# Attention logits of a pair of heads in the two row halves of TensorE, without copied q and k

## The chip, the cores and the metric

The kernel runs on one core of a Trainium2 chip. The metric is the device time of one execution in microseconds (us); lower is better. Times of several runs are given as a median with the lowest and the highest.

## What is computed

A trunk of two decoder layers on 512 tokens of width 1024. Each layer is a mixer (attention) and a SwiGLU feed-forward, each behind an RMS norm and with a residual add. Layer 0 mixes with 16 heads of width 64, 8 of them with a merged dilated-window pattern and 8 plainly causal at this length. Layer 1 is differential attention: 8 heads, each with two maps of queries and keys of width 64 and values of width 128. Of it the part that matters here is this:

```
qh = q.reshape(B, S, H, 2, HEAD_DIM).transpose(0, 2, 3, 1, 4)
kh = k.reshape(B, S, H, 2, HEAD_DIM).transpose(0, 2, 3, 1, 4)
...
logits = jnp.einsum('bhiqd,bhikd->bhiqk', qc, kh).astype(jnp.float32) * ATTN_SCALE
logits = jnp.where(kpos[None, :] <= qpos[:, None], logits, NEG_INF)
p = jax.nn.softmax(logits, axis=-1)
attn = p[:, :, 0] - lam * p[:, :, 1]
```

## The kernel before

Everything is kept transposed, features on the 128 partitions and the 512 tokens along the free dimension. Each large operand is split into a high and a low part (float32r), and a product of two operands is made of three matmuls: high by high, high by low and low by high (`mm3`, line 420). The `z` of a tile's shape `[128, 2, 512]` is that part.

**Weights** arrive as slabs of 128 x 1024. A slab lands raw in `wraw` (2 buffers) by a transfer of SP's queue. ScalarE writes the high part to `whl`, and the low part is made either by a subtraction on VectorE or GpSimd (`slab`, line 370) or by a second, accumulating transfer that POOL's queue issues (`slab_acc`, line 381). `whl` has 3 buffers (line 274). One slab feeds 24 matmuls of 128 x 512.

**The mixer** (line 561) works in pairs of heads: a tile of 128 rows holds head 0 of the pair in rows 0 to 63 and head 1 in rows 64 to 127. `qk_gemm` (line 615) projects one q or k tile, and `qk_rope` (line 622) rotates it and splits it into `st`, high and low. `pair_qk` (line 632) then copies within the on-chip memory, by SP's queue: for each head of the pair, `q2` holds that head's 64 rows twice, in both row halves, for both parts (2 x 2 transfers of 256 KB), and `k2` holds the high part of k in the upper half of the rows and the low part in the lower half (2 x 2 transfers of 128 KB). So one matmul over 128 rows multiplies one part of q by both parts of k.

`logits` (line 655) makes one block of 128 queries by w = 128, 256, 384 or 512 keys for one head, with two such matmuls into a `ps_s` bank (2 banks). VectorE then adds the mask and takes the row's extremum in one instruction (line 662), and ScalarE makes the exponential with its sum. `transposes` (line 670) turns the block round on TensorE and splits it into `pt`. Then follow the products with the values into `ps_o`. `att_plain` (line 686, layer 0) goes through all blocks of one head, makes that head's value product, and then does the other head. `att_diff` (line 711, layer 1) takes both heads' logits of a block together, since it subtracts one map from the other. The output projection follows (line 769), two of whose slabs (`XTRA`) are split into `q2` buffers by `slab_in` (line 391).

**The order of the work** is set by a planner in the kernel (`Sched.run`, line 96), when the program is built. It goes through all operations of the trunk with a table of costs, gives each a rank by the longest way that is left behind it, and at each step issues, on the engine that can start first, the ready operation with the highest rank. A buffer is given out in the order of use, and only when the last user of its earlier content is done by the planner's clock. The order in which mixer steps enter is written out by hand (`ORDER`, line 214: Q is a pair's q and k, V a group of values, A a pair's attention). Each engine then runs its instructions in the planned order, so projections of later pairs stand between the products of an attention.

Of the kernel before, what the change touches and what calls it, by code (L numbers as in the profile page):

```python
# [10 lines left out]
F32 = mybir.dt.float32  # L11
# [51 lines left out]
class Sched:  # L63
# [7 lines left out]
    def buf(self, tag):  # L71
        b = Buf(tag, len(self.queue[tag]))
        self.queue[tag].append(b)
        return b
# [178 lines left out]
def trunk(ctx, tc, xT, pos, consts_in, gv, lamv, wv0, wqk0, wo0, wgu0, wd0, wv1, wqk1, wo1, wgu1, wd1, out):  # L253
# [8 lines left out]
    def tag(name, shape, dt, n, scope=0):  # L262
        tags[name] = (scope, n)
        shapes[name] = (shape, dt)

    R5 = [128, 512]
# [4 lines left out]
    tag("acc", R5, F32, 1)  # L271
    tag("sq", R5, F32, 2)
    tag("wraw", [128, 1024], F32, 2)
    tag("whl", [128, 2, 1024], F32R, 3)
    tag("cc", [128, 640], F32, 1)
    tag("onesr", [128, 128], F32R, 1)
    tag("gvt", [128, 73], F32, 1)
# [6 lines left out]
    for L in range(2):  # L284
        sc = AT[L]
        for n, shp, dt, c in (("v", [128, 4, 2, 256], F32R, 2), ("sh", R5, F32, 2), ("a", R5, F32, 2),
                              ("st", [128, 2, 512], F32R, 2), ("q2", [128, 2, 512], F32R, 4),
                              ("k2", R5, F32R, 4), ("lg", R5, F32, 4),
                              ("pt", [128, 2, 1664], F32R, 2), ("of", R5, F32, 1),
                              ("ot", [128, 2, 512], F32R, 8), ("col", [128, 4], F32, 8)):  # L290
            tag(f"{n}{L}", shp, dt, c, sc)
        if L == 1:
            tag("ss1", [128, 2, 512], F32R, 1, sc)
        else:
            tag("ma0", R5, F32, 1, sc)
        sc = FF[L]
        for n, shp, dt, c in (("ht", [128, 2, 512], F32R, NF), ("rbc", R5, F32, 1), ("gs", R5, F32, 3),
                              ("us", R5, F32, 3)):
            tag(f"{n}{L}", shp, dt, c, sc)
# [6 lines left out]
    def dma(dst, src, r, w, nbytes):  # L306
        op([("S", 520)], lambda e: nc.sync.dma_start(dst(), src()), r, w, dma=nbytes)
# [253 lines left out]
    def mixer(L, wv, wqk, wo, gi_next):  # L561
# [53 lines left out]
        def qk_gemm(i):  # L615
            w = slab(wqk[i], 1024) if L + i == 0 else slab_acc(wqk[i])
            p = buf("ps_s" if L + i == 0 else "ps_g")
            for c in range(NC):
                mm3(p, w, c, xop, c, c == 0, c == NC - 1)
            return p  # L620

        def qk_rope(p):
            P = [(p, None)]
            sh, a, st = buf(f"sh{L}"), buf(f"a{L}"), buf(f"st{L}")
            op([("V", vtt(512))], lambda e: V.stream_shuffle(sh.t, p.t, swap), P, [(sh, None)])  # L625
            tt("V", lambda: a.t, lambda: p.t, lambda: ck.t, OP.mult, 512, P + [(ck, None)], [(a, None)])
            tt("GV", lambda: sh.t, lambda: sh.t, lambda: sk.t, OP.mult, 512, [(sk, None)], [(sh, None)])
            tt("GV", lambda: a.t, lambda: a.t, lambda: sh.t, OP.add, 512, [(sh, None)], [(a, None)])
            split(lambda: st.t[:, 0, :], lambda: st.t[:, 1, :], lambda: a.t, 512, [(a, None)], (st, 0), (st, 1))
            return st  # L630

        def pair_qk(i):
            q = qk_rope(early.pop() if early else qk_gemm(2 * i))
            q2, k2 = [], []
            for b in range(2):
                t = buf(f"q2{L}")
                for z in range(2):
                    dma(lambda t=t, z=z: t.t[z * 64:z * 64 + 64].bitcast(F32),
                        lambda b=b: q.t[b * 64:b * 64 + 64].bitcast(F32), [(q, 0), (q, 1)], [(t, z)], 2 ** 18)
                q2.append(t)  # L640
            k = qk_rope(qk_gemm(2 * i + 1))
            for b in range(2):
                t = buf(f"k2{L}")
                for z in range(2):
                    dma(lambda t=t, z=z: t.t[z * 64:z * 64 + 64].bitcast(F32),
                        lambda b=b, z=z: k.t[b * 64:b * 64 + 64, z, :].bitcast(F32), [(k, z)], [(t, z)], 2 ** 17)
                k2.append(t)
            return q2, k2

        ot = {}  # L650

        mask_b = (lambda: cc.t[:, 128:640]), (cc, None)
        mask_a = (lambda: ma.t), (ma, None)

        def logits(q2, k2, i, mask):
            w = (i + 1) * 128
            p, lg, col = buf("ps_s"), buf(f"lg{L}"), buf(f"col{L}")
            P = [(p, None)]
            for z in range(2):
                mm(lambda: p.t[:, :w], lambda z=z: q2.t[:, z, i * 128:i * 128 + 128], lambda: k2.t[:, :w], w,  # L660
                   z == 0, z == 1, [(q2, 0), (q2, 1), (k2, 0), (k2, 1)], P)
            op([("V", vtt(w) + 10)], lambda e: V.tensor_tensor_reduce(  # L662
                lg.t[:, :w], p.t[:, :w], mask[0]()[:, 512 - w:], -0.125, 3.0e38, OP.add, OP.min,
                col.t[:, 0:1]), P + [mask[1]], [(lg, None), (col, 0)])
            func(lambda: lg.t[:, :w], lambda: lg.t[:, :w], AF.Exp, w, SET + [(col, 0)], [(lg, None), (col, 1)],
                 scale=-1.0, bias=lambda: col.t[:, 0:1], accum=lambda: col.t[:, 1:2], extra=2)
            op([("V", 76)], lambda e: V.reciprocal(col.t[:, 2:3], col.t[:, 1:2]), [(col, 1)], [(col, 2)])
            return lg, col
# [14 lines left out]
            tt("V", lambda: dst(1), p3, lambda: dst(0).bitcast(F32), OP.subtract, w, P + [(pt, (i, 0))],  # L683
               [(pt, (i, 1))])

        def att_plain(hp, q2, k2):
            o = buf(f"of{L}")
            for b in range(2):
                pt = buf(f"pt{L}")
                for i in range(4):  # L690
                    lg, col = logits(q2[b], k2[b], i, mask_a if hp < 4 else mask_b)
                    w = (i + 1) * 128
                    copy("VA", lambda lg=lg, w=w: lg.t[:, :w], lambda lg=lg, w=w: lg.t[:, :w], w, [(col, 2)],
                         [(lg, None)], scale=lambda col=col: col.t[:, 2:3], extra=1)
                    transposes(lg, i, pt)
                po = buf("ps_o")
                v, q = vt[hp]
                for j in range(4):
                    for z in range(2):
                        mm(lambda j=j, po=po: po.t[:, j * 128:],  # L700
                           lambda j=j, b=b: v.t[:, j, q, b * 128:b * 128 + 128],
                           lambda j=j, z=z, pt=pt: pt.t[:, z, j * 512:j * 384 + 512], 512 - 128 * j,
                           j == 0 and z == 0, j == 3 and z == 1,
                           [(v, (j, 0)), (v, (j, 1))] + [(pt, (i, z)) for i in range(j, 4)], [(po, None)])
                oh = lambda b=b: o.t[b * 64:b * 64 + 64]
                copy("A", oh, lambda b=b, po=po: po.t[64 - b * 64:128 - b * 64], 512, [(po, None)], [(o, b)], psum=True)
                tt("V", oh, lambda b=b, po=po: po.t[b * 64:b * 64 + 64], oh, OP.add, 512, [(po, None)], [(o, b)])
            t = ot[hp] = buf(f"ot{L}")
            split(lambda: t.t[:, 0, :], lambda: t.t[:, 1, :], lambda: o.t, 512, [(o, 0), (o, 1)], (t, 0), (t, 1))

        def att_diff(hp, q2, k2):
            pt = buf(f"pt{L}")
            for i in range(4):
                w = (i + 1) * 128
                l0, c0 = logits(q2[0], k2[0], i, mask_b)
                l1, c1 = logits(q2[1], k2[1], i, mask_b)
                tt("V", lambda c1=c1: c1.t[:, 3:4], lambda c1=c1: c1.t[:, 2:3], lambda: sm.t[:, 20:21], OP.mult, 1,
                   [(c1, 2), (sm, "nlam")], [(c1, 3)])
                copy("VA", lambda l1=l1, w=w: l1.t[:, :w], lambda l1=l1, w=w: l1.t[:, :w], w, [(c1, 3)],
                     [(l1, None)], scale=lambda c1=c1: c1.t[:, 3:4], extra=1)  # L720
                stt(lambda l0=l0, w=w: l0.t[:, :w], lambda l0=l0, w=w: l0.t[:, :w], lambda c0=c0: c0.t[:, 2:3],
                    lambda l1=l1, w=w: l1.t[:, :w], OP.mult, OP.add, w, [(c0, 2), (l1, None)], [(l0, None)])
                transposes(l0, i, pt)
# [44 lines left out]
                S_.boost = 0.0  # L768
        for n in range(NC):
            if n in XTRA:  # L770
                w = slab_in(wo[n], f"q2{L}")
                p = buf("ps_t")
            else:
                w = slab_acc(wo[n])
                p = buf("ps_g")

            def oop(c):
                t = ot[c]
                return (lambda: t.t[:, 0, :]), (t, 0), (lambda: t.t[:, 1, :]), (t, 1)
            for c in range(NC):  # L780
                mm3(p, w, c, oop, c, c == 0, c == NC - 1)
            residual(p, n)
            operand(n, gi_next)
            square(n, "GV")
# [258 lines left out]
```

## Time and profile before

| what | value |
|---|---|
| median of 3 runs | 1264.34 us (1262.17 to 1268.2) |
| the profiled execution | 1265.66 us |
| its span, first to last instruction | 1263.9 us |
| mean granted clock of TensorE | 0.986 |
| moved by DMA | 163.81 MB |

The span has five stages: the start with the loads of x (0 to 20 us), the mixer of layer 0 (20 to 270), the feed-forward of layer 0 (270 to 631), the mixer of layer 1 (631 to 889) and the feed-forward of layer 1 with the final norm (889 to the end). Names to the left of an arrow are written, names to the right are read; L349 and L352 are the helpers that record matmuls and transposes, so tiles tell what a row is about. In the profile `q<-st` and `k<-st` are the copies into `q2` and `k2`.

### The profile page before, as it was taken

The numbers are of one execution on the slowest core, as the hardware profiler recorded it, in microseconds if no ns is written. First come the engines' busy times: TensorE is split into PE (matmuls) and PEld (weight loads), VectorE is DVE, ScalarE is ACT, GpSimd is POOL, SyncE is SP. The second block draws the span as 40 slices with busy tenths as digits, with TensorE's granted clock in tenths as the row PEclk, the third lists the DMA queues.
The fourth block names the chain that finished last, engine by engine and source line by source line (L and its number), as shares of the span: only waits on it lengthen the run. The fifth ranks groups of instructions, "written<-read, shape, count | busy, mean of one in ns | idle before, by whom it ended". The sixth has DMA issues, their size and how long they took to land.

```text
span 1263.9 us, 16077 instructions
## 1 busy us (share of the span) xinstructions
PE 1218.3 (96%) x5994; PEld 1024.9 (81%) x5994; DVE 646.3 (51%) x1348; ACT 581.5 (46%) x1005; POOL 179.3 (14%) x161
## 2 busy tenths in 40 slices
PE   7799999999999999999999998899999999999997
PEld 6688788888888888888887786787888888888887
DVE  7558586644444444333236885785444444442233
ACT  6468686742233322332346796786332223332231
POOL 4222242320000000000022443422100000000000
PEclk9999999999999999999999998999999999999998
DMA  5968898443323333333479968756233332333332
GB/s 181 242 148 193 196 214 185 101 117 100 95 91 98 100 100 92 95 92 92 119 170 219 221 152 191 175 134 151 83 100 100 100 96 91 99 96 92 104 92 67
DMA packets 52237, 163.81 MB, mean 130 GB/s; under 512 B 6848, under 2 KB 10048, under 8 KB 52160
## 3 DMA queue, kind: packets, MB, share of 16 engines
q1 hardware_dynamic: 43952, 132.90, 36.2%
q0 software_dynamic: 8208, 29.89, 13.3%
q8 instruction: 47, 0.77, 0.3%
q14 instruction: 30, 0.25, 0.1%
HBM read 135.50 MB, written 2.10 MB: 109 GB/s over the span
## 4 chain that ended last, share of the span: by engine, by line
PE 51%; issue 32%; DMA 6%; DVE 6%; ACT 3%; POOL 1%; POOLq 0%; SPq 0%; DVEq 0%; ACTq 0%
PE ps_g L349 44%; DMA whl<-wv 3%; PE ps_s L349 3%; PE ps_o L349 2%; DMA k<-st 2%; PE ps_t L352 1%; DMA whl<-wqk 1%; DVE lg L662 1%; PE ps_t L349 1%; DVE lg L322 1%; ACT whl L318 1%; DMA whl<-wo 1%; DVE sh L625 1%; DVE lg L330 1%; ACT lg L344 0%
## 5 line engine op out<-in xcount | busy, mean ns | idle before, releaser
L349 PE MATMUL ps_g<-xo,whl 128*128 128x512 f32 x2856 | 677.9, 393 | 3.7 <-DMA whl<-wqk 3.7
L349 PEld LDWEIGHTS ps_g<-xo,whl 128*128 128x128 f32 x2856 | 532.4, 189 | 111.7 <-DMA whl<-wqk 5.2
L318 ACT ACTIVATE whl<-wraw 128x1024 fp32r<-128x1024 f32 (+2 forms) x259 | 261.2, 1023 | 506.5 <-PE ps_g L349 400.4
L349 PE MATMUL ps_g<-ht,whl 128*128 128x512 f32 (+1 forms) x1122 | 241.3, 377 | 0.0
L349 PEld LDWEIGHTS ps_g<-ht,whl 128*128 128x128 f32 x1122 | 202.0, 188 | 38.6
L327 DVE TENSOR_TENSOR whl<-wraw,whl 128x1024 fp32r<-128x1024 f32 (+1 forms) x136 | 162.1, 1192 | 122.8 <-ACT whl L318 122.8
L349 PE MATMUL ps_g<-whl,xo 128*128 128x256 f32 x744 | 108.7, 296 | 13.6 <-DMA whl<-wv 8.0
L349 PEld LDWEIGHTS ps_g<-whl,xo 128*128 128x128 f32 x744 | 100.4, 200 | 18.0 <-DMA whl<-wv 9.1
L327 DVE TENSOR_TENSOR us<-ps_g,rbc 128x512 f32<-128x512 f32 x44 | 30.4, 692 | 141.1 <-PE ps_g L349 141.1
L327 DVE TENSOR_TENSOR gs<-ps_g,rbc 128x512 f32<-128x512 f32 x44 | 30.4, 692 | 98.7 <-PE ps_g L349 93.0
L344 ACT ACTIVATE lg<-lg,col 128x128 f32<-128x128 f32 (+3 forms) x128 | 70.9, 556 | 11.2 <-DVE col L662 10.2
L349 PE MATMUL ps_g<-ot,whl 128*128 128x512 f32 x288 | 73.9, 396 | 1.7 <-DMA whl<-wo 1.1
L349 PE MATMUL ps_s<-k,q 128*128 128x128 f32 (+3 forms) x256 | 62.7, 342 | 10.6 <-issue 7.1
L387 POOL DMA_DIRECT2D whl<-wv x14 | 12.2, 873 | 361.2 <-ACT whl L318 361.1
L349 PEld LDWEIGHTS ps_g<-ot,whl 128*128 128x128 f32 x288 | 52.6, 188 | 12.2 <-DMA whl<-wo 1.5
L349 PEld LDWEIGHTS ps_s<-k,q 128*128 128x128 f32 x256 | 44.8, 203 | 19.4 <-issue 8.4
L327 POOL TENSOR_TENSOR fo<-h,rbc 128x256 f32<-128x256 f32 x4 | 2.9, 732 | 363.6 <-ACT rbc L318 363.6
L662 DVE CUSTOM_DVE_ANT_0 lg<-ps_s,cc 128x128 f32<-128x128 f32 (+3 forms) x96 | 45.6, 484 | 17.0 <-PE ps_s L349 14.6
L327 DVE TENSOR_TENSOR h<-ps_g,h 128x512 f32<-128x512 f32 (+1 forms) x29 | 19.1, 672 | 64.9 <-PE ps_g L349 64.9
L327 DVE TENSOR_TENSOR pt<-ps_t,pt 128x128 fp32r<-128x128 f32 (+1 forms) x96 | 45.3, 481 | 4.2 <-ACT pt L318 3.7
L352 PE MATMUL ps_t<-cc,lg 128*128 128x128 f32 x240 | 41.7, 276 | 4.2 <-DVE lg L330 3.4
L318 ACT ACTIVATE pt<-ps_t 128x128 fp32r<-128x128 f32 (+1 forms) x96 | 40.4, 431 | 11.1 <-PE ps_t L352 10.0
(129 smaller groups left out, 1011.4 us busy)
## 6 DMA issues: line engine op xcount, KB each, us to landing
wraw<-wgu SPq DMA_DIRECT2D x88, 512.0 KB, 3.5
wraw<-wqk SPq DMA_DIRECT2D x32, 512.0 KB, 7.0
q<-st SPq DMA_DIRECT2D x64, 256.0 KB, 7.5
wraw<-wd SPq DMA_DIRECT2D x32, 512.0 KB, 3.5
whl<-wqk POOLq DMA_DIRECT2D x31, 512.0 KB, 7.8
k<-st SPq DMA_DIRECT2D x64, 128.0 KB, 5.2
wraw<-wo SPq DMA_DIRECT2D x16, 512.0 KB, 5.6
wraw<-wv SPq DMA_DIRECT2D x14, 512.0 KB, 6.1
```

The source lines that it names most:

```text
L318: A.activation(out_(), in_(), AF.Copy, scale=sc)
L322: V.tensor_scalar(out_(), in_(), sc, None, OP.mult)
L327: lambda e: E[e].tensor_tensor(out_(), a(), b(), o), r, w)
L330: op([("V", vtt(n, 1))], lambda e: V.scalar_tensor_tensor(out_(), a(), s(), b(), o0, o1), r, w)
L344: A.activation(out_(), in_(), f, scale=scale, **kw)
L349: lambda e: T.matmul(out_(), l(), r_(), start=start, stop=stop), r, w)
L352: op([("T", 108)], lambda e: T.transpose(out_(), in_(), ident()), r + [(cc, None)], w)
L387: op([("G", 1100)], lambda e: G.dma_start(w.t[:, 1, :], src, accum_op=OP.add), [(w, (1, 0))], [(w, (1, 0))], dma=2 * 1024 * 512)
L625: op([("V", vtt(512))], lambda e: V.stream_shuffle(sh.t, p.t, swap), P, [(sh, None)])
L662: op([("V", vtt(w) + 10)], lambda e: V.tensor_tensor_reduce(lg.t[:, :w], p.t[:, :w], mask[0]()[:, 512 - w:], -0.125, 3.0e38, OP.add, OP.mi ...
```

## The change

The logits read q and k where the rotation leaves them, in `st`. For head b of the pair a matmul uses the 64 rows b*64 to b*64+63 of both operands, and writes that head's `ps_s` bank. There are three of them for a head (high by high, high by low, low by high) where there were two over 128 rows; the product of the two low parts is no longer made. The six of a pair's block are recorded in turn, head 0 and head 1, and both `ps_s` banks are taken at once. In the planner's table one of them costs max(128, w) / 4.4 ns, where one over 128 rows costs max(256, w) / 2.4 + 3. The copies `q2` and `k2` and their transfers are gone; `st` has 6 buffers instead of 2, and `whl` 4 instead of 3. In layer 0 the two heads of a pair now go block by block together, each with its own `pt`, and both value products stand behind them. The two `XTRA` slabs are split into `st` buffers.

```diff
--- before.py
+++ after.py
@@ -271,7 +271,7 @@
     tag("acc", R5, F32, 1)
     tag("sq", R5, F32, 2)
     tag("wraw", [128, 1024], F32, 2)
-    tag("whl", [128, 2, 1024], F32R, 3)
+    tag("whl", [128, 2, 1024], F32R, 4)
     tag("cc", [128, 640], F32, 1)
     tag("onesr", [128, 128], F32R, 1)
     tag("gvt", [128, 73], F32, 1)
@@ -284,8 +284,7 @@
     for L in range(2):
         sc = AT[L]
         for n, shp, dt, c in (("v", [128, 4, 2, 256], F32R, 2), ("sh", R5, F32, 2), ("a", R5, F32, 2),
-                              ("st", [128, 2, 512], F32R, 2), ("q2", [128, 2, 512], F32R, 4),
-                              ("k2", R5, F32R, 4), ("lg", R5, F32, 4),
+                              ("st", [128, 2, 512], F32R, 6), ("lg", R5, F32, 4),
                               ("pt", [128, 2, 1664], F32R, 2), ("of", R5, F32, 1),
                               ("ot", [128, 2, 512], F32R, 8), ("col", [128, 4], F32, 8)):
             tag(f"{n}{L}", shp, dt, c, sc)
@@ -631,34 +630,28 @@
 
         def pair_qk(i):
             q = qk_rope(early.pop() if early else qk_gemm(2 * i))
-            q2, k2 = [], []
-            for b in range(2):
-                t = buf(f"q2{L}")
-                for z in range(2):
-                    dma(lambda t=t, z=z: t.t[z * 64:z * 64 + 64].bitcast(F32),
-                        lambda b=b: q.t[b * 64:b * 64 + 64].bitcast(F32), [(q, 0), (q, 1)], [(t, z)], 2 ** 18)
-                q2.append(t)
-            k = qk_rope(qk_gemm(2 * i + 1))
-            for b in range(2):
-                t = buf(f"k2{L}")
-                for z in range(2):
-                    dma(lambda t=t, z=z: t.t[z * 64:z * 64 + 64].bitcast(F32),
-                        lambda b=b, z=z: k.t[b * 64:b * 64 + 64, z, :].bitcast(F32), [(k, z)], [(t, z)], 2 ** 17)
-                k2.append(t)
-            return q2, k2
+            return q, qk_rope(qk_gemm(2 * i + 1))
 
         ot = {}
 
         mask_b = (lambda: cc.t[:, 128:640]), (cc, None)
         mask_a = (lambda: ma.t), (ma, None)
 
-        def logits(q2, k2, i, mask):
+        def logits(q, k, i, mask):
             w = (i + 1) * 128
-            p, lg, col = buf("ps_s"), buf(f"lg{L}"), buf(f"col{L}")
+            ps = [buf("ps_s") for b in range(2)]
+            for n, (y, z) in enumerate(((0, 0), (0, 1), (1, 0))):
+                for b in range(2):
+                    rows = slice(b * 64, b * 64 + 64)
+                    mm(lambda b=b: ps[b].t[:, :w], lambda y=y, rows=rows: q.t[rows, y, i * 128:i * 128 + 128],
+                       lambda z=z, rows=rows: k.t[rows, z, :w], w, n == 0, n == 2, [(q, y), (k, z)], [(ps[b], None)],
+                       cost=max(128, w) / 4.4)
+            return [soft(ps[b], w, mask) for b in range(2)]
+        def soft(p, w, mask):
+            lg, col = buf(f"lg{L}"), buf(f"col{L}")
             P = [(p, None)]
-            for z in range(2):
-                mm(lambda: p.t[:, :w], lambda z=z: q2.t[:, z, i * 128:i * 128 + 128], lambda: k2.t[:, :w], w,
-                   z == 0, z == 1, [(q2, 0), (q2, 1), (k2, 0), (k2, 1)], P)
             op([("V", vtt(w) + 10)], lambda e: V.tensor_tensor_reduce(
                 lg.t[:, :w], p.t[:, :w], mask[0]()[:, 512 - w:], -0.125, 3.0e38, OP.add, OP.min,
                 col.t[:, 0:1]), P + [mask[1]], [(lg, None), (col, 0)])
@@ -683,16 +676,16 @@
             tt("V", lambda: dst(1), p3, lambda: dst(0).bitcast(F32), OP.subtract, w, P + [(pt, (i, 0))],
                [(pt, (i, 1))])
 
-        def att_plain(hp, q2, k2):
+        def att_plain(hp, q, k):
             o = buf(f"of{L}")
-            for b in range(2):
-                pt = buf(f"pt{L}")
-                for i in range(4):
-                    lg, col = logits(q2[b], k2[b], i, mask_a if hp < 4 else mask_b)
-                    w = (i + 1) * 128
+            pts = [buf(f"pt{L}") for b in range(2)]
+            for i in range(4):
+                w = (i + 1) * 128
+                for (lg, col), pt in zip(logits(q, k, i, mask_a if hp < 4 else mask_b), pts):
                     copy("VA", lambda lg=lg, w=w: lg.t[:, :w], lambda lg=lg, w=w: lg.t[:, :w], w, [(col, 2)],
                          [(lg, None)], scale=lambda col=col: col.t[:, 2:3], extra=1)
                     transposes(lg, i, pt)
+            for b, pt in enumerate(pts):
                 po = buf("ps_o")
                 v, q = vt[hp]
                 for j in range(4):
@@ -708,12 +701,11 @@
             t = ot[hp] = buf(f"ot{L}")
             split(lambda: t.t[:, 0, :], lambda: t.t[:, 1, :], lambda: o.t, 512, [(o, 0), (o, 1)], (t, 0), (t, 1))
 
-        def att_diff(hp, q2, k2):
+        def att_diff(hp, q, k):
             pt = buf(f"pt{L}")
             for i in range(4):
                 w = (i + 1) * 128
-                l0, c0 = logits(q2[0], k2[0], i, mask_b)
-                l1, c1 = logits(q2[1], k2[1], i, mask_b)
+                (l0, c0), (l1, c1) = logits(q, k, i, mask_b)
                 tt("V", lambda c1=c1: c1.t[:, 3:4], lambda c1=c1: c1.t[:, 2:3], lambda: sm.t[:, 20:21], OP.mult, 1,
                    [(c1, 2), (sm, "nlam")], [(c1, 3)])
                 copy("VA", lambda l1=l1, w=w: l1.t[:, :w], lambda l1=l1, w=w: l1.t[:, :w], w, [(c1, 3)],
@@ -768,7 +760,7 @@
                 S_.boost = 0.0
         for n in range(NC):
             if n in XTRA:
-                w = slab_in(wo[n], f"q2{L}")
+                w = slab_in(wo[n], f"st{L}")
                 p = buf("ps_t")
             else:
                 w = slab_acc(wo[n])
```

## Rows read from the trace of the kernel before

**Rows 1.** The page, part 1: busy time, share of the span, instructions.
```profile
PE 1218.3 (96%) x5994; PEld 1024.9 (81%) x5994; DVE 646.3 (51%) x1348; ACT 581.5 (46%) x1005; POOL 179.3 (14%) x161
```

**Rows 2.** Mixer windows: length, PE, PEld, DVE, ACT, POOL busy, PEclk, DMA share, GB/s.
```profile
20.00:270.00 250.00, 236.32 (x1328) 203.35 (x1329) 159.30 (x476) 167.39 (x354) 69.10 (x62) 0.99 0.75 175
...
631.00:889.00 258.00, 239.92 (x1298) 204.56 (x1297) 168.76 (x462) 178.59 (x352) 88.58 (x75) 0.97 0.76 175
```

**Rows 3.** Waits of TensorE, 20 to 889 us: total us, times, longest.
```profile
PE ps_g L349 <- DMA whl<-wv: 8.0, 4, 3.6
PE ps_s L349 <- issue: 7.1, 3, 6.0
PE ps_g L349 <- DMA whl<-wqk: 3.7, 3, 1.7
PE ps_s L349 <- DMA k<-st: 3.4, 1, 3.4
```

**Rows 4.** Timeline of TensorE at the two waits for copies.
```profile
59.39 1.19 PE L349 MATMUL ps_s<-k,q 128*128 128x128 f32 x4 [5.95 <-issue]
...
771.99 0.66 PE L349 MATMUL ps_s<-k,q 128*128 128x128 f32 x2 [3.40 <-DMA k<-st]
```

**Rows 5.** Chain of waits, 45 to 87 and 755 to 776: start, us, what.
```profile
45.88 10.95 DMA k<-st
...
761.72 9.65 DMA k<-st
```

**Rows 6.** Windows behind three waits, columns as in rows 2.
```profile
59.40:64.00 4.60, 4.60 (x18) 4.41 (x19) 3.02 (x13) 2.83 (x8) 1.35 (x1) 0.50 1.06 221
...
768.60:772.00 3.40, 0.01 (x1) 0.04 (x1) 1.29 (x2) 1.21 (x2) 0.00 (x0) 0.83 1.10 219
772.00:781.00 9.00, 8.05 (x23) 6.49 (x24) 5.03 (x19) 4.60 (x12) 3.25 (x3) 0.50 1.01 231
...
822.00:825.00 3.00, 3.00 (x17) 3.00 (x16) 1.29 (x3) 1.88 (x4) 0.00 (x0) 0.51 1.05 228
```

**Rows 7.** The page, part 6: DMA issues, count, KB each, us to landing.
```profile
wraw<-wqk SPq DMA_DIRECT2D x32, 512.0 KB, 7.0
q<-st SPq DMA_DIRECT2D x64, 256.0 KB, 7.5
...
whl<-wqk POOLq DMA_DIRECT2D x31, 512.0 KB, 7.8
k<-st SPq DMA_DIRECT2D x64, 128.0 KB, 5.2
```

**Rows 8.** Timeline of TensorE, 160.9 to 168 and 675 to 682.
```profile
160.97 0.62 PE L349 MATMUL ps_s<-k,q 128*128 128x128 f32 x4
161.43 1.08 PE L349 MATMUL ps_g<-xo,whl 128*128 128x512 f32 x4
...
166.05 0.38 PE L352 MATMUL ps_t<-cc,lg 128*128 128x128 f32 x2
166.19 0.48 PE L349 MATMUL ps_g<-xo,whl 128*128 128x512 f32 x1
...
167.06 0.63 PE L349 MATMUL ps_s<-k,q 128*128 128x512 f32 x2
167.53 0.63 PE L349 MATMUL ps_g<-xo,whl 128*128 128x512 f32 x2
...
676.12 0.63 PE L349 MATMUL ps_s<-k,q 128*128 128x256 f32 x4
676.59 0.85 PE L349 MATMUL ps_g<-xo,whl 128*128 128x512 f32 x3
677.28 0.87 PE L349 MATMUL ps_s<-k,q 128*128 128x384 f32 x4
677.99 0.87 PE L349 MATMUL ps_g<-xo,whl 128*128 128x512 f32 x3
```

**Rows 9.** The page, part 5: the projections' products and their loads.
```profile
L349 PE MATMUL ps_g<-xo,whl 128*128 128x512 f32 x2856 | 677.9, 393 | 3.7 <-DMA whl<-wqk 3.7
L349 PEld LDWEIGHTS ps_g<-xo,whl 128*128 128x128 f32 x2856 | 532.4, 189 | 111.7 <-DMA whl<-wqk 5.2
```

**Rows 10.** Line 662, instructions on VectorE: duration ns min/median/max.
```profile
L662 DVE CUSTOM_DVE_ANT_0 lg<-ps_s,cc x96: 278/478/692, 162.0 to 843.7; 128x128 f32<-128x128 f32 x24, 128x256 f32<-128x256 f32 x24, 128x384 f32<-128x384 f32 x24, 128x512 f32<-128x512 f32 x24
```

## The prediction

> **What bounds the kernel now.** I read the page's engine table first: TensorE is busy for 96% of the span [rows 1], so what counts is its idle time and its own work. The windows by stage show where the idle time is: 13.7 us in the attention of layer 0 and 18.1 us in that of layer 1 [rows 2]; the same rows show the transfers busy for three quarters of both stages, VectorE and ScalarE for two thirds. The reader should see two saturated things side by side there, TensorE and the DMA engines. The table of TensorE's waits names what ended that idle time [rows 3]: weight slabs (wv 8.0 us, wqk 3.7 us), and 10.5 us ahead of logits, 7.1 put down to "issue" and 3.4 to the copies of k. The timeline has the long one of each kind, 5.95 us before 59.39 and 3.40 us before 771.99 [rows 4]. The chain of waits shows the copies of k under both: one step of 10.95 us and one of 9.65 us [rows 5], though a copy of k takes 5.2 us at the median [rows 7]; I read the "issue" as the rest of the wait for copies. The windows just behind show the further price: the granted clock is at 0.50, the lower level (1.2 GHz), for 4.60 us of work and then 8.05 us, and 0.51 for 3.00 us behind a wait for wv [rows 6].
>
> **The copies go.** 64 copies of q at 256 KB and 64 of k at 128 KB [rows 7] are 25 MB, against the 89 MB that the two stages move (250 and 258 us at 175 GB/s [rows 2]): over a quarter of their traffic, and 128 entries on SP's queue. Everything that stands behind them there are weight loads, so these start earlier. The waits for copies go: 7.1 + 3.4 = **-10.5 us** of idle time, and with them the stretches at the lower clock, half of 4.60 + 8.05 us = **-6.3 us**. What is late next: the logits then wait for the split of k into st on ScalarE and VectorE, which the copies waited for anyway, so nothing is added. POOL's queue loses nothing; its accumulating weight loads only share the DMA engines with less.
>
> **The fourth weight buffer, and the lighter queue.** What they can take away is the weight waits, 8.0 + 3.7 us, and half of the 3.00 us at low clock: 13.2 us [rows 3, 6]. The other end is nothing: TensorE reaches the same weights 10 us earlier, so a slab that came just in time is late by as much. A slab has two transfers in a row, 7.0 and 7.8 us [rows 7], in stages with busy DMA engines; a quarter less traffic and one slab more in flight both help. I take the middle, **-6.6 us**. In the feed-forward stages no wait for weights is listed inside, so the buffer is worth nothing there.
>
> **The logits.** Before, one block of 128 queries has four products for the pair (two a head). Start to next start, the four take 0.46 us at 128 columns, 0.47 at 256, 0.71 at 384, and the two of one head 0.47 at 512, so 0.94 for four [rows 8]. A pair costs 2.58 us, 16 pairs 41.3 us. Now there are six products on 64 rows each; q's low half times k's low half is left out. Three prices:
> - Both halves side by side, loads too: three slots for four, 0.75 of 41.3, **-10.3 us**.
> - One after the other: six for four, **+20.6 us**.
> - Between: products side by side, weight loads one after the other. At 128 columns a product takes 0.115 us though 256 take hardly more (0.47/4) [rows 8]: below 256 columns something other than the columns sets the pace, which I take to be the load of the stationary block that each product has. Six at 0.115 are 0.69 us, three slots at 512 columns 0.70: 0.69 + 0.69 + 0.69 + 0.70 = 2.77 us a pair, **+3.1 us**.
>
> I take the last, since the 128-column row is the nearest one to six short products with a load each. The Trainium skill (TensorE: Matmul & The Clock Gate, Part 3, The mechanism) says that a load overlaps running products when the row groups differ; by that the first price would hold and the sum would be 13.4 us lower, and no row here has a product on part of the rows.
>
> **The change of form.** Products on 64 rows stand between products on 128 rows: 16 pairs x 4 blocks, in and out, 128 changes at least. The trace has no such change. Its nearest row is the change from products to transposes and back, which shows no gap (two transposes in 0.14 us, then the next product [rows 8]): nothing, my value. The other end: the engine finishes one form before it begins the other. A product lasts 0.393 us [rows 9] while the next starts 0.23 us later (three from 676.59 to 677.28 [rows 8]), so 0.16 us of it lies under its successor, and a load takes 0.189 us [rows 9]; with both uncovered a change costs 0.35 us, 45 us in all. A gain is excluded: a change does no work.
>
> **Order and buffers.** Both ps_s banks are now taken by one call, so block i+1 cannot start before VectorE has read block i; those reads take 0.28 to 0.69 us [rows 10]. Layer 1 already worked in that manner (both heads' products of a block come together [rows 8]), and the projection's products fill the time, so I put it at nothing. In layer 0 the two heads now run abreast and their value products meet at one ps_o bank; projections cover that too, except behind the last pair, where some us may be lost. The st buffers (6) hold three pairs, as the order needs. If the cover of projections were gone, the price would be one read per block, at most 0.69 us for each of 64.
>
> **Sum.** Against the profiled execution, 1265.66 us (span 1263.9, some 1.8 around it; 1.3 above the median of 1264.34): 1265.66 - 10.5 - 6.3 - 6.6 + 3.1 = 1245.4. I forecast 1245 us.
>
> **Rivals.**
> - *Everything overlaps.* Loads and products run abreast and the weight waits vanish: 1265.66 - 10.5 - 6.3 - 13.2 - 10.3 = 1225 us. For it: the traffic that goes. Against: DMA engines at 1.0 and above in the waits [rows 6] can still be late.
> - *The halves don't run side by side*, so the change doesn't do what it says: 1265.66 - 23.4 + 20.6 = 1263 us, no change. It can come from the engine, or from the order: the planner books each product at about half its time, and the second bank comes free up to 0.69 us behind the first [rows 10], so one head's three products may be put alone. For it: no row shows two products at once. Against: at 128 columns both banks are free at the start of a pair.
> - *The engine is emptied at every change of form*, which ends on the other side. Its place is each of the 128 changes, its price up to 0.35 us. The gains of 20.3 us are used up at 0.16 us a change; at 0.28 us the time is 1245 + 36 = 1281 us, at 0.35 us 1290. Against: the transposes. For it: nothing in the rows forbids it, and a wait for emptying would hide nowhere, as TensorE is the bound. The Trainium skill (TensorEngine Tiling (Array Packing), Key Properties) says just this, that switching between tiling modes drains the engine; no run here shows it yet.
>
> **How the numbers follow.** The forecast has 0.46, everything overlapping 0.18, no side by side 0.17, emptying 0.19. Half a percent (1258 to 1270.7 us) is about what a measurement of this kernel can tell from no change. The forecast and the first rival are faster, with a little of the second: 0.66. The second rival mostly lies within: 0.15. Emptying is slower: 0.19. The range goes from the first rival, 1225, past the second to the foot of the third, 1272; the forecast's own range, with the weight waits from nothing to all, is 1239 to 1252.
>
> **What would show it.** Right: no wait ahead of ps_s for copies, the two stretches at 0.50 gone, wv and wqk waits of some 6 us left, DMA share of both stages near 0.55, and six logits products of a block within 0.7 us. If blocks of 512 columns take 0.70 us, products overlap; at 1.4 us they don't. If the projection's product behind a group of logits starts 0.2 to 0.35 us late each time, the engine is emptied. The forecast is wrong if wv and wqk waits grow past 13 us, or if logits in layer 0 lead to waits of transposes for lg.

## The result and the profile after

The changed kernel takes 1274.16 us (median of 5 runs, 1273.97 to 1274.97) against 1264.34 us; the ratio is 1.0073, 95% interval 1.0049 to 1.0098. It is slower by 0.7%, some 9 to 10 us, where 1245 us was forecast, and lies 2 us above the range.

The page of the changed kernel, part 1, beside [rows 1]:

```profile
PE 1254.0 (99%) x6122; PEld 1021.7 (80%) x6122; DVE 642.7 (51%) x1337; ACT 583.9 (46%) x1009; POOL 188.2 (15%) x168
```

Its windows over the two mixers, columns as in [rows 2]:

```profile
20.00:270.00 250.00, 248.13 (x1359) 198.06 (x1360) 157.90 (x466) 171.52 (x358) 70.41 (x64) 0.99 0.54 123
638.00:892.00 254.00, 252.16 (x1339) 197.51 (x1338) 163.45 (x457) 173.66 (x346) 91.89 (x78) 1.00 0.55 125
```

And all its waits of TensorE over 0.6 us, in the whole span, beside [rows 3]:

```profile
PE ps_g L348 <- DVE xo L329: 5.8, 4, 2.8
PE ps_o L348 <- DVE small L329: 1.3, 1, 1.3
PE ps_t L351 <- DVE lg L329: 1.3, 1, 1.3
PE ps_t L897 <- DVE small L912: 1.2, 1, 1.2
PE ps_t L351 <- DVE pt L326: 0.7, 2, 0.3
```

The waits are gone, for copies and for weights: TensorE's idle time in the mixers is 1.9 and 1.8 us where it was 13.7 and 18.1, the share of the transfers fell from 0.75 and 0.76 to 0.54 and 0.55, the granted clock is 0.99 and 1.00, the full level (2.4 GHz). In the whole span TensorE idles 1272.4 - 1254.0 = 18.4 us, before 45.6. And yet the span grew by 8.5 us: TensorE's busy time grew by 35.7 us, at a mean clock of 0.994 instead of 0.986. The question is what keeps TensorE busy for longer.

The timeline of TensorE in the changed kernel shows it (start, us from start to end of the run, count last):

```profile
88.28 0.79 PE L348 MATMUL ps_s<-st,st 64*128 64x384 f32 x3
89.00 0.33 PE L351 MATMUL ps_t<-cc,lg 128*128 128x128 f32 x1
...
180.84 0.55 PE L348 MATMUL ps_s<-st,st 64*128 64x128 f32 x6
181.31 1.18 PE L348 MATMUL ps_g<-xo,whl 128*128 128x512 f32 x4
182.42 0.64 PE L348 MATMUL ps_s<-st,st 64*128 64x256 f32 x6
182.99 1.20 PE L348 MATMUL ps_g<-xo,whl 128*128 128x512 f32 x4
184.12 0.80 PE L348 MATMUL ps_s<-st,st 64*128 64x384 f32 x6
184.84 0.50 PE L348 MATMUL ps_g<-xo,whl 128*128 128x512 f32 x1
...
186.66 0.96 PE L348 MATMUL ps_s<-st,st 64*128 64x512 f32 x3
187.55 0.50 PE L348 MATMUL ps_g<-xo,whl 128*128 128x512 f32 x1
187.98 0.73 PE L348 MATMUL ps_s<-st,st 64*128 64x512 f32 x2
...
189.23 0.50 PE L348 MATMUL ps_s<-st,st 64*128 64x512 f32 x1
```

Two things are to be seen. Six products at 384 columns take 0.72 us (184.12 to 184.84), and three of one head alone take 0.72 us as well (88.28 to 89.00): the halves run abreast where both heads stand together. But every group of them carries something extra: three at 512 take 0.89 us (186.66 to 187.55), and the lone projection product behind them 0.43 us (to 187.98), where one such product takes 0.23 [rows 8]. And the groups are many: the block at 512 keys is cut into three here (3, 2 and 1 products), and of the 384 products the trace has 121 groups, not 64. Only 26 of the 64 blocks stand whole, as six; 43 groups hold three products, 52 another number.

The same stretch with the weight loads (PEld), in brackets how long the load path idled before:

```profile
186.66 0.53 PEld L348 LDWEIGHTS ps_s<-st,st 64*128 64x128 f32 x3 [0.36 <-DVE col L655]
186.66 0.96 PE L348 MATMUL ps_s<-st,st 64*128 64x512 f32 x3
...
187.55 0.19 PEld L348 LDWEIGHTS ps_g<-xo,whl 128*128 128x128 f32 x1 [0.36 <-issue]
187.55 0.50 PE L348 MATMUL ps_g<-xo,whl 128*128 128x512 f32 x1
...
187.98 0.29 PEld L348 LDWEIGHTS ps_s<-st,st 64*128 64x128 f32 x2 [0.24 <-issue]
```

At each change the first load and its product begin together, behind a gap of the load path: the load no longer goes ahead under the product before it. So it is at all 242 changes of this trace: the first load starts at most 3 ns ahead of its product, where the first loads of the logits and of the product behind them led by 0.19 and 0.17 us at the median before.

### The profile page after: what moved, and what is told of

Same layout as the page of the kernel before. It is cut to its first block, busy times and chain, and to the rows that moved or that the text cites. A ratio compares the mean times of both kernels' runs of the same rounds, so it can differ in the third digit from the quotient of the medians.

```text
span 1272.4 us, 15989 instructions
## 1 busy us (share of the span) xinstructions
PE 1254.0 (99%) x6122; PEld 1021.7 (80%) x6122; DVE 642.7 (51%) x1337; ACT 583.9 (46%) x1009; POOL 188.2 (15%) x168
## 3 DMA queue, kind: packets, MB, share of 16 engines
q0 software_dynamic: 8208, 29.89, 13.7%
## 4 chain that ended last, share of the span: by engine, by line
PE 93%; DVE 4%; issue 1%; ACT 1%; DMA 0%; SPq 0%; POOLq 0%; POOL 0%; DVEq 0%; ACTq 0%
PE ps_g L348 80%; PE ps_s L348 6%; PE ps_o L348 3%; PE ps_t L351 2%; PE ps_t L348 2%; DVE lg L329 1%; DVE a L326 1%; DVE a L333 0%; ACT whl L317 0%; DVE sh L624 0%; DVE xo L329 0%; DVE lg L321 0%; DVE pt L326 0%; DVE sh L329 0%; DMA posi<-pos 0%
## 5 line engine op out<-in xcount | busy, mean ns | idle before, releaser
L348 PEld LDWEIGHTS ps_g<-whl,xo 128*128 128x128 f32 x744 | 96.4, 194 | 13.5 <-DVE xo L329 6.7
L348 PE MATMUL ps_s<-st,st 64*128 64x128 f32 (+3 forms) x384 | 76.4, 361 | 0.0
L348 PEld LDWEIGHTS ps_s<-st,st 64*128 64x128 f32 x384 | 41.6, 184 | 29.8 <-issue 14.5
L317 ACT ACTIVATE pt<-ps_t 128x128 fp32r<-128x128 f32 (+3 forms) x96 | 40.9, 429 | 28.0 <-PE ps_t L351 26.9
L326 POOL TENSOR_TENSOR sh<-sh,sk 128x512 f32<-128x512 f32 x30 | 40.5, 1351 | 84.7 <-DVE sh L624 50.0
L326 DVE TENSOR_TENSOR pt<-ps_t,pt 128x128 fp32r<-128x128 f32 (+3 forms) x96 | 45.9, 483 | 9.2 <-ACT pt L317 9.0
```

Source lines behind the costliest of these rows:

```text
L317: A.activation(out_(), in_(), AF.Copy, scale=sc)
L326: lambda e: E[e].tensor_tensor(out_(), a(), b(), o), r, w)
L348: lambda e: T.matmul(out_(), l(), r_(), start=start, stop=stop), r, w)
```

## The experiments

The theory from here on: each change between products on 64 and on 128 rows costs TensorE about 0.2 us, there are 242 of them, and the halves do run abreast. The rivals: six loads and products are the price in themselves; or the halves never run abreast.

**All rows, same order.** The planner sees no difference, so the order of every engine stays as it was.

```diff
-                    rows = slice(b * 64, b * 64 + 64)
+                    rows = slice(0, 128)
```

> The changed kernel with its six products of a block on all 128 rows of both operands, in the same order and number: each logits block then sums both heads (the separation of the two heads is left out). Theory, each change between products on 64 and on 128 rows costs about 0.2 us, 242 of them for 121 groups: they go, some 48 us, and what ran abreast in two halves runs in turn, some 19 us more: about 1245 us. Rival, the six loads and six products themselves are the price, whatever the rows: no gain, 1274 us or above. Rival, the halves never run abreast: nothing is lost with the halves, so 1226 us.

Measured: 1248.37 us (ratio to the kernel before 0.987, 0.9833 to 0.9906). The timeline at the same products as above:

```profile
178.12 1.23 PE L348 MATMUL ps_s<-st,st 128*128 128x384 f32 x6
...
179.01 0.19 PEld L348 LDWEIGHTS ps_g<-xo,whl 128*128 128x128 f32 x1
...
179.19 0.39 PE L348 MATMUL ps_g<-xo,whl 128*128 128x512 f32 x1
...
180.58 0.65 PEld L348 LDWEIGHTS ps_s<-st,st 128*128 128x128 f32 x3
...
180.81 0.85 PE L348 MATMUL ps_s<-st,st 128*128 128x512 f32 x3
...
181.27 0.19 PEld L348 LDWEIGHTS ps_g<-xo,whl 128*128 128x128 f32 x1
...
181.50 0.39 PE L348 MATMUL ps_g<-xo,whl 128*128 128x512 f32 x1
181.50 0.42 PEld L348 LDWEIGHTS ps_s<-st,st 128*128 128x128 f32 x2
181.73 0.62 PE L348 MATMUL ps_s<-st,st 128*128 128x512 f32 x2
```

Each load now starts 0.18 to 0.23 us ahead of its product, also at the ends of a group. Three at 512 take 0.69 instead of 0.89 us and the projection product behind them 0.23 instead of 0.43: 0.40 us a group, 48 us for 121. The order is the same in both runs, so all groups can be laid side by side: a group takes 0.19 us longer on 64 rows whether it holds three of one head's products at 512 columns (0.89 and 0.70 us at the median) or one (0.43 and 0.23), and the products on all rows ahead of it and behind it take 0.10 us longer each. So the price belongs to the group and not to each product; 0.20 us a change is half of what going in and out costs together. Six at 384 take 1.07 instead of 0.72, the overlap that is lost. Both rivals fall: with as many loads and products the time fell by 26 us, and it did not fall to 1226.

**Both heads in the same half.**

```diff
-                    rows = slice(b * 64, b * 64 + 64)
+                    rows = slice(0, 64)
```

> The changed kernel with both heads' products on rows 0 to 63, in the same order and number: the second head's logits are then a repeat of the first's (the second head is left out). Theory, products on different halves run abreast where they stand together: groups of six lose it, 10 to 19 us more, 1284 to 1293 us. Rival, the halves never run abreast, or the loads set the price: no change, 1274 us.

Measured: 1288.84 us (1.0194, 1.0157 to 1.0231), 15 us above the changed kernel. Its timeline:

```profile
185.09 0.88 PE L348 MATMUL ps_s<-st,st 64*128 64x128 f32 x6
185.90 1.20 PE L348 MATMUL ps_g<-xo,whl 128*128 128x512 f32 x4
187.03 0.98 PE L348 MATMUL ps_s<-st,st 64*128 64x256 f32 x6
187.94 1.19 PE L348 MATMUL ps_g<-xo,whl 128*128 128x512 f32 x4
189.06 1.31 PE L348 MATMUL ps_s<-st,st 64*128 64x384 f32 x6
190.30 0.50 PE L348 MATMUL ps_g<-xo,whl 128*128 128x512 f32 x1
...
192.10 0.96 PE L348 MATMUL ps_s<-st,st 64*128 64x512 f32 x3
193.00 0.49 PE L348 MATMUL ps_g<-xo,whl 128*128 128x512 f32 x1
193.42 0.73 PE L348 MATMUL ps_s<-st,st 64*128 64x512 f32 x2
```

Six at 128, 256 and 384 columns take 0.81, 0.91 and 1.24 us where the two halves took 0.47, 0.57 and 0.72. So the two halves run abreast, their loads too. Three of one head at 512 columns and the lone projection product behind them take 0.90 and 0.42 us, in the changed kernel 0.89 and 0.43: a change costs the same with one half alone, so it is the number of rows that counts.

**Six products as one operation.** The planner may take two buffers of a kind for one operation, and takes the six only when both banks are free.

```diff
-                            if b.seq != head[t] or not free[t] or (sc > cur and sum(
+                            m = new[t] = new.get(t, -1) + 1
+                            if b.seq != head[t] + m or len(free[t]) <= m or (sc > cur and sum(
...
+            op([("T", 6 * max(128, w) / 4.4)], six, [(q, 0), (q, 1), (k, 0), (k, 1)], [(x, None) for x in ps])
```

> The changed kernel with the six products of a block planned as one operation that needs both banks free, at the sum of their old costs: 64 groups of products on 64 rows instead of 121. Theory, a change of form costs about 0.2 us and the halves run abreast: 57 groups fewer at 0.4 us are 23 us, and the groups that held one head now hold both in the same time, some 11 us more: about 1240 us. Rival, the halves never run abreast: six products in turn, about 1270 us. Rival, the six loads are the price: no change, 1274 us. Against all: waiting for both banks could add waits of TensorE.

Measured: 1243.53 us (0.9833, 0.979 to 0.9875). The timeline of one pair:

```profile
151.68 0.55 PE L650 MATMUL ps_s<-st,st 64*128 64x128 f32 x6
152.16 1.20 PE L350 MATMUL ps_g<-xo,whl 128*128 128x512 f32 x4
153.28 0.62 PE L650 MATMUL ps_s<-st,st 64*128 64x256 f32 x6
153.83 1.66 PE L350 MATMUL ps_g<-xo,whl 128*128 128x512 f32 x6
...
155.64 0.79 PE L650 MATMUL ps_s<-st,st 64*128 64x384 f32 x6
156.36 1.19 PE L350 MATMUL ps_g<-xo,whl 128*128 128x512 f32 x4
...
159.07 0.97 PE L650 MATMUL ps_s<-st,st 64*128 64x512 f32 x6
159.97 0.50 PE L350 MATMUL ps_g<-xo,whl 128*128 128x512 f32 x1
```

A pair's groups take 0.48 + 0.55 + 0.72 + 0.90 = 2.65 us; less 0.20 us each for leaving the form, 1.85 us are left of products, against 2.58 before. Putting both heads together, with the order that follows from it, is worth 31 us. But the changes still have their price: with 0.20 us more for each group on the way in and behind it, a pair costs TensorE 3.45 us, 14 us more for 16 pairs than the 2.58 before. So on TensorE the halves don't pay even here; this kernel is 21 us faster than the one before because TensorE waits less (1243.3 - 1219.0 = 24.3 us, before 45.6) and works less at the lower clock (some 9 us, before 25). The waits of transposes for lg rose from 1.3 to 4.9 us; that this is the price of waiting for both banks was not tested by itself.

**Three weight buffers.**

```diff
-    tag("whl", [128, 2, 1024], F32R, 4)
+    tag("whl", [128, 2, 1024], F32R, 3)
```

> The changed kernel with 3 weight buffers as before. Theory, the copies' traffic and their place in SP's queue made the weight waits, the fourth buffer is worth little: 1274 to 1278 us, waits for wv and wqk under 3 us. Rival, the fourth buffer took the 11.7 us of weight waits and the clock behind them away: 1284 us or more, with waits for wv and wqk near those of the kernel before.

Measured: 1284.94 us (1.0175, 1.0127 to 1.0222), 11 us above the changed kernel: the theory had this too low, and the time is the rival's, though with less than half of the waits that the rival named. Its waits for weights:

```profile
PE ps_g L348 <- DMA whl<-wv: 2.6, 3, 1.5
PE ps_g L348 <- DMA whl<-wqk: 2.3, 3, 1.6
...
PE ps_g L348 <- DMA whl<-wo: 0.7, 1, 0.7
```

They come back by 5.6 us, 4.9 of it for wv and wqk where [rows 3] had 11.7, and TensorE's busy time is 3.7 us longer, of which three more groups (124) explain 1.2. The rest stays open.

**The copies again, unread.** The kernel with three weight buffers, and on SP's queue 128 copies of the old sizes into two spare buffers.

```diff
+                    dma(lambda t=t, z=z: t.t[z * 64:z * 64 + 64].bitcast(F32),
+                        lambda b=b: q.t[b * 64:b * 64 + 64].bitcast(F32), [(q, 0), (q, 1)], [(t, z)], 2 ** 18)
...
+                    dma(lambda t=t, z=z: t.t[z * 64:z * 64 + 64, 0, :].bitcast(F32),
+                        lambda b=b, z=z: k.t[b * 64:b * 64 + 64, z, :].bitcast(F32), [(k, z)], [(t, z)], 2 ** 17)
```

> The changed kernel with 3 weight buffers and, on SP's queue, the 128 copies of q and k in their old sizes again, into two spare buffers that nothing reads. Against the run with 3 weight buffers (1284.94 us). Theory, the copies' traffic and places in SP's queue made about half of the weight waits: waits for wv, wqk and wo go from 5.6 us to some 12 us, and the time to 1291 to 1295 us. Rival, the buffer alone decides on these waits: 1283 to 1287 us, with weight waits of 5 to 6 us.

Measured: 1293.24 us (1287.11 to 1297.05; 1.0257, 1.0225 to 1.0289). The median lies where the theory has it, but its mechanism isn't shown. The profiled execution was the fastest of the six, and its weight waits, 4.0 us for wv, 3.2 for wqk and 0.5 for wo, are 7.7 us, only 2.1 above the run without copies, where some 12 were expected. The copies cost some 8 us in the median. About half of that goes with the clock: the spans are 1285.3 us at a mean granted clock of 0.996, 1287.3 at 0.994, 1291.3 to 1292.0 at 0.991 and 0.990, and 1295.3 at 0.987, and the run without copies has 1282.2 and 1283.0 at 0.994 and 1291.3 at 0.987. So at the same clock some 4 to 5 us are left. What lowers it, and where the rest lies, this profile does not show.

**Three groups a pair.** On the kernel with six products as one: blocks 0 and 2 (128 and 384 keys) go one behind the other into the same two banks.

```diff
+        GROUPS = ((0, 2), (1,), (3,))
...
+                            T.matmul(ps[b].t[:, o:o + w], q.t[rows, y, i * 128:i * 128 + 128], k.t[rows, z, :w],
...
```

> The kernel of the run with six products planned as one, with the products of blocks 0 and 2 (128 and 384 keys) put one behind the other into the same two banks: three groups a pair instead of four, 48 instead of 64. Theory, each group costs 0.4 us for its two changes: 16 groups fewer are 6 to 7 us, about 1237 us. Rival, the price lies in the products themselves: no change, 1243 us. Against both: the longer chain from two blocks to the softmax adds waits of TensorE for lg, then above 1243 us.

Measured: 1235.22 us (0.9794, 0.9767 to 0.9821), the fastest of all. The timeline, with twelve products in a group:

```profile
168.59 1.12 PE L654 MATMUL ps_s<-st,st 64*128 64x128 f32 x12
169.65 2.33 PE L350 MATMUL ps_g<-xo,whl 128*128 128x512 f32 x9
171.91 0.62 PE L654 MATMUL ps_s<-st,st 64*128 64x256 f32 x6
172.46 0.74 PE L350 MATMUL ps_g<-xo,whl 128*128 128x512 f32 x2
```

The twelve take 1.06 us where the two groups took 0.48 + 0.72 = 1.20; with the 0.20 us on the way into and behind a group that is not made, that is 0.34 us for each of 16 pairs, 5.4 of the 8 us. The waits for lg fell from 4.9 to 3.2 us. The intervals of the two ratios overlap a little, but the traces agree with the gain: TensorE's busy time fell from 1219.0 to 1213.0 us. A pair costs it 1.06 + 0.55 + 0.90 us and 0.20 for each of three groups, 3.11 us, which is still 8.5 us more for 16 pairs than before the change.

**True costs in the planner.** On the kernel with six products as one.

```diff
-            op([("T", 6 * max(128, w) / 4.4)], six, [(q, 0), (q, 1), (k, 0), (k, 1)], [(x, None) for x in ps])
+            op([("T", {1: 690, 2: 760, 3: 930, 4: 1100}[i + 1])], six, [(q, 0), (q, 1), (k, 0), (k, 1)], [(x, None) for x in ps])
```

> The kernel of the run with six products planned as one, with the planner's cost of such a group set to what it took there with both changes (0.69, 0.76, 0.93 and 1.10 us instead of 0.17 to 0.70): same 64 groups. Theory, TensorE is the bound and its work is unchanged: 1240 to 1245 us. Rival, the wrong cost spoils the order (waits for lg of 4.9 us): those waits go, 1238 us.

Measured: 1246.65 us (0.9883, 0.9858 to 0.9908), 2 us above what the theory gave. The order is no better: waits for lg are 6.3 us. The rival falls.

## Why the prediction was wrong

**The copies and the weights: right in kind, and larger than forecast.** The wait for copies went with its stretches at 0.50, the wv and wqk waits went altogether (half was taken), and the DMA share is the 0.55 that was named. The three terms summed to -23.4 us, clock included; measured are -27.2 us of idle time and some 9 us of clock (TensorE was busy for 24.9 us at the lower level before and for 7.3 after, half of the difference), -36 in all. What was named next did not come late: waits of transposes for lg are 1.3 us. How much of this the fourth buffer brought and how much the copies is only known from the changed kernel (11 and some 8 us); no run has the old logits with four weight buffers.

**The logits: the wrong price.** "Weight loads one after the other", +3.1 us, was taken because of the 128-column row. With six together the products take 1.85 us a pair against 2.58, -11.7 us before the price of the changes: the first price, which had loads abreast as well. The Trainium skill (TensorE: Matmul & The Clock Gate, Part 3, The mechanism) says that a load overlaps running products when the row groups differ; the runs with two halves and with one (0.47 and 0.81 us for six at 128) agree. In the changed kernel this gain did not arrive, since one head's three products often stand alone.

**The change of form: the step that failed.** It was put at nothing, by the transposes, which are on 128 rows and so no change of this kind. It costs 0.20 us, inside the bounds of 0 and 0.35. And 128 was called the least number; it is 242, because the planner cut the groups. That cut stood only under the second rival ("one head's three products may be put alone"): the second bank comes free a mask read later than the first, and the first head's three are put in at once. That reason is argued from the planner's rule, and it can't be the only one: the 46 groups of one or two products show that other work was also put between the products of one head. Six planned as one operation rule out both, and the 64 groups come back. The changes come to 242 x 0.20 = 48 us. The third rival had the mechanism and its break-even, 0.16 us a change, and a chance of 0.19. The Trainium skill (TensorEngine Tiling (Array Packing), Key Properties) says that a change of tiling mode drains the engine. This trace agrees: a change costs 0.20 us, and no load goes ahead across it.

**The sum again:** the 121 groups take 67.9 us from their first start to the next product's start, the 107 groups before took 47.2. Of these 1.8 us were idle and 6.4 lay at the lower clock, so some 42 to 43 us are left at full clock and without waits, and the groups cost 25 us more. With 0.20 us more for each of the 121 on the way in and behind it, that is 25 + 24 = 49 us. Against it stand 27 us of idle time and 9 of clock: +13, measured +8.5 in the span. The step that failed is large enough to turn the forecast gain into a loss; some 5 us are not accounted for.

## What to carry to other kernels

Before products are put on part of the rows, count how often they will stand between products on all rows: here each such change cost 0.2 us, and whole groups, planned as one operation with both banks free, turned a loss of 0.7% into a gain of 1.7%, and fewer groups into one of 2.1%. Even then the products on 64 rows cost TensorE more than the ones that they replaced (14 and 8.5 us); the gain is that of the copies and waits that they made needless. A planner that prices a product as though its partner always ran beside it can still part the two, and did so here in 38 of 64 blocks. And where transfers keep TensorE waiting, the time behind a wait at the lower clock belongs to the price.

## What was not expected of the hardware

- A weight load did not go ahead under the product before it when the number of rows changed: a gap of 0.24 to 0.36 us on the load path, 0.20 us of TensorE at each change, the same with one half as with two.
- Within a group, loads and products of two halves ran abreast in full: six at 128 columns in 0.48 us with a change in it, 0.81 us in one half.
- The fourth weight buffer was worth 11 us by itself in the changed kernel, though the waits that it removed sum to 5.6 us.
